# A streaming-encoder trunk on one core: four tiles side by side in the first pass, the first norm by tokens, a last tile split over fewer rows, and buffers at other places

## The chip, the cores and the metric

The kernel runs on one core of one Trainium2 chip. The metric is the device time of one execution in microseconds (us). Before the change the median of three runs is 1658.42 us (1656.04 to 1658.62).

## What is computed

One layer of a token mixer on x of 256 tokens and 2048 features, followed by an MLP and a last norm. Cut to its core the reference is:

```
h = rmsnorm(x, g1)
z = h @ w_in + b_in                      # 7 parts of 2048: xa, ya, cb, cc, cx, ga, gb
xa = rg_lru(causal_conv4(xa) + conv_a_b) # gates by 8 blocks of 256, a forward scan
out_a = (xa * gelu(ya)) @ w_pa
out_b = (cb * causal_conv3(cc * cx)) @ w_pb
x = x + (sigmoid(ga) * out_a + sigmoid(gb) * out_b) @ w_o
u = relu(rmsnorm(x, g2) @ w_mlp1) ** 2   # 8192 wide
out = rmsnorm(x + u @ w_mlp2, final_g)
```

Everything is float32.

## The kernel before

Features lie on the 128 partitions, tokens along the free side. x is kept as `x[128, 16, 256]`: 16 rows k of 128 features, 256 tokens each. Each operand of a product is split in two float32r parts, hi (a cast, on ACT) and lo (what the cast lost, on DVE); a buffer like `xg[128, 16, 2, 256]` holds both. A weight tile is 128 outputs wide; its weights for 8 rows k are a slab of 128 x 1024 numbers (512 KB). `Weights.make` loads a slab into a `raw` buffer with one DMA on SP's queue and splits it into `whi` and `wlo`; `take` keeps three slabs ahead of the one in use, in four buffers each. A row of a product is a pair of matmuls: hi weights against hi and lo data side by side (512 columns), lo weights against hi data (256 columns), both into one PSUM bank (`psz`, six of them). A tile of a z part is 16 such pairs, 32 for the second MLP product.

The tile framework puts the instructions of each engine in an order by priority; `high_priority(AHEAD)` draws the splits forward. Each engine then works through its own list in order, and so do the DMA queues.

The parts that the change touches:

- **The beginning.** x comes in eight pieces of two rows with quarters of two tiles' slabs between them (`load_x`, `W.make(2, 4, ...)`). The norm's factor is one number per token and is applied after the product (`z_done` multiplies by `rs`), so PE can start on x scaled by g1 alone. `first_pair` does the two xa tiles side by side, row by row; the two ya tiles follow one after the other from whole slabs; these four are the early tiles. `first_norm` squares x on ACT in eight parts, adds them up on DVE, sums over partitions with matmuls by `ones` (`total`), and takes the inverse root of 128 x 256 numbers (`rsqrt`).
- **The merged branches** `mg` (128 x 16 x 2 x 256, in a pool of its own, `big2`) are streamed by the w_o product (16 tiles) and, reused for `u`, by half of the rows of the second MLP product's second part (15 tiles and the last one). All other products but the small gate ones stream a `big` buffer, of which there are three.
- **The end.** The last tile (feature row 15, 32 rows k) is done in two halves of 128 tokens. After each half its squares complete the sum of squares of all features (`ssq` holds the others'), a short chain on one column gives the scale of its tokens (`scale_of`), a matmul spreads it over the partitions (`spread`), and `store` multiplies 16 feature rows by it and writes them out, 512 bytes for each feature and half.

Of the kernel before, what the change touches and what calls it, by code (L numbers as in the profile page):

```python
# [9 lines left out]
F32 = mybir.dt.float32  # L10
# [28 lines left out]
class Weights:  # L39
# [8 lines left out]
    def make(self, n=1, parts=1, before=None):  # L48

        nc = self.nc  # L50
        w = HALF * P // parts
        got = [(self.slabs[len(self.made) + m],
                self.raw_pool.tile([P, HALF * P], F32, name="raw"),
                self.hi_pool.tile([P, HALF * P], F32R, name="whi"),
                self.lo_pool.tile([P, HALF * P], F32R, name="wlo")) for m in range(n)]
        for i in range(parts):
            c = slice(i * w, (i + 1) * w)
            if before is not None:
                before(i)
            for src, raw, hi, lo in got:  # L60
                nc.sync.dma_start(raw[:, c], src[:, c])  # L61
                with self.tc.high_priority(AHEAD):
                    nc.scalar.copy(hi[:, c], raw[:, c])  # L63
                    nc.vector.tensor_tensor(lo[:, c], raw[:, c], hi[:, c].bitcast(F32), ALU.subtract)  # L64
        self.made += [(hi, lo) for _, _, hi, lo in got]
# [19 lines left out]
def trunk(ctx: ExitStack, tc: tile.TileContext, xT, par, w_in, w_lru, w_pa, w_pb, w_o, w_1, w_2, out):  # L85
# [40 lines left out]
    pr = keep.tile([P, NPAR], F32, name="pr")  # L126

# [18 lines left out]
    sink = keep.tile([P, 1], F32, name="sink")  # L146
    nc.scalar.copy(sink, eps)
# [21 lines left out]
    xg = big.tile([P, NT, 2, S], F32R, name="big")  # L169

# [76 lines left out]
    def first_pair():  # L247

        w = W.first(4)
        two = [psz.tile([P, 2, S], F32, name="psz") for _ in range(2)]  # L250
        for k in range(NT):
            for m in range(2):
                hi, lo = w[k // HALF * 2 + m]
                c = slice(k % HALF * P, (k % HALF + 1) * P)
                nc.tensor.matmul(two[m], hi[:, c], xg[:, k], start=k == 0, stop=False)  # L255
                nc.tensor.matmul(two[m][:, 1, :], lo[:, c], xg[:, k, 0, :], start=False, stop=k == NT - 1)
        return two

    early = first_pair() + [z_product() for m in range(2)]

    def first_norm(pool):
        parts = [pool.tile([P, 2, S], F32, name=n) for n in ("xc", "gy", "cb", "cc", "gate0", "gate1", "q", "v")]
        for k in range(HALF):
            nc.scalar.activation(parts[k], x[:, 2 * k:2 * k + 2, :], AF.Square, scale=pc("one", 0))
        n = HALF // 2
        while n:
            for k in range(n):
                nc.vector.tensor_tensor(parts[k], parts[k], parts[n + k], ALU.add)
            n //= 2
        rsqrt(rs, [parts[0][:, 0, :], parts[0][:, 1, :]])  # L270
# [3 lines left out]
    with tc.tile_pool(name="w1", bufs=1) as w1:  # L274
        first_norm(w1)
        for g in range(NB):
# [33 lines left out]
            if g == 0:  # L310
                decay()
# [34 lines left out]
    big2 = ctx.enter_context(tc.tile_pool(name="big2", bufs=1, reuse_waits="tile"))  # L346
    mg = big2.tile([P, NT, 2, S], F32R, name="mg")
# [43 lines left out]

    w = [W.take() for _ in range(4)]
    eye = pr[:, OFF["eye"]:OFF["eye"] + P]
    col = {}

    def sum_of(th):

        ps = psl.tile([P, 512], F32, name="psl")
        nc.tensor.matmul(ps[:, 0:1], ssq[:, th * P:(th + 1) * P], ones[:, 0:1], start=True, stop=False)
        return ps  # L400

    def half(th, between):
        c = slice(th * P, (th + 1) * P)
        ps = psz.tile([P, 2, S], F32, name="psz")
        for k in range(4 * HALF):
# [5 lines left out]
            nc.tensor.matmul(ps[:, :, :P], hi[:, b], a, start=k == 0, stop=False)  # L411
# [26 lines left out]
    def spread(d):  # L438

        ps = psl.tile([P, 1, 512], F32, name="psl")  # L440
        nc.tensor.matmul(ps[:, 0, :P], ones, d[:, :P], start=True, stop=True)
        return ps[:, :, :P]
# [64 lines left out]
```

## Time and profile before

| | |
|---|---|
| median of 3 runs | 1658.42 us (1656.04 to 1658.62) |
| the profiled execution, own time | 1657.99 us |
| its span, first to last instruction | 1656.1 us |
| PE busy | 1637.5 us (99%), 9490 matmuls |
| DVE, ACT busy | 68%, 52% |
| DMA | 312 MB, mean 189 GB/s |

The span is shorter than the execution's time by what lies around the first and last instruction. Times in rows are counted from the span's start. PE is TensorE's matmuls (their ends are modelled, so two that follow one another overlap in the rows, and their starts are the better measure), DVE VectorE, ACT ScalarE, SPq the DMA queue that SyncE issues. What stands in square brackets behind a row is the idle time of the engine ahead of it and what ended it.

### The profile page before, as it was taken

The page shows a single profiled execution, that of the slowest core. Times are in us where ns is not written, and L with a number is a line of the kernel's source. Part 1 is how long each engine was busy: PE and PEld are TensorE (multiplying, and loading weights), DVE is VectorE, ACT ScalarE, POOL GpSimd, SP SyncE. Part 2 cuts the span into 40 slices and gives each one's busy share as a digit, 9 for nine tenths or more (in the row PEclk, how much of TensorE's full clock was granted, in tenths as well). Part 3 has the DMA queues.
Part 4 walks back from the last instruction along what each step waited for, and adds up shares of the span by engine and source line. Part 5 has one row for each costly group of instructions (what it writes and reads, how often), then busy time and mean ns, then how long its engine had stood idle before and what let it go on. Part 6 is the DMA issues. An engine that isn't in the chain of part 4 may idle for free.

```text
span 1656.1 us, 24430 instructions
## 1 busy us (share of the span) xinstructions
PE 1637.5 (99%) x9490; PEld 1440.7 (87%) x9490; DVE 1130.7 (68%) x1645; ACT 867.7 (52%) x1275; POOL 3.4 (0%) x37
## 2 busy tenths in 40 slices
PE   8999999999999999999999999999999999999997
PEld 6888888888888888888888888888888888888886
DVE  6989779878977666666667666665555777755554
ACT  7666666666665444444455544444443444444443
POOL 0000000000000000000000000000000000000000
PEclk9999999999999999999999999999999999999998
DMA  8565555555555555555555555555555555555552
GB/s 257 181 192 190 191 192 190 187 192 192 186 186 193 190 191 191 191 191 190 190 183 189 185 189 190 189 191 190 190 191 190 191 190 191 188 188 188 189 190 90
DMA packets 91604, 312.21 MB, mean 189 GB/s; under 512 B 9952, under 2 KB 16224, under 8 KB 91488
## 3 DMA queue, kind: packets, MB, share of 16 engines
q1 hardware_dynamic: 91488, 310.66, 57.7%
q8 instruction: 74, 1.21, 0.3%
q14 instruction: 42, 0.34, 0.1%
HBM read 308.52 MB, written 2.10 MB: 188 GB/s over the span
## 4 chain that ended last, share of the span: by engine, by line
PE 97%; DMA 1%; DVE 1%; ACT 0%; SPq 0%; issue 0%; DVEq 0%; ACTq 0%
PE psz L225 62%; PE psz L226 32%; DMA raw<-w_in_s 1%; DVE wlo L64 1%; PE psz L411 0%; PE psl L319 0%; PE psl L320 0%; PE psl L321 0%; DMA pr<-par 0%; ACT whi L63 0%; PE psz L412 0%; DVE x L447 0%; SPq L61 0%; SPq L172 0%; PE psl L154 0%
## 5 line engine op out<-in xcount | busy, mean ns | idle before, releaser
L225 PE MATMUL psz<-big,whi 128*128 128x512 f32 x4048 | 1407.1, 392 | 1.6 <-ACT whi L63 1.2
L226 PE MATMUL psz<-big,wlo 128*128 128x256 f32 x4048 | 1133.5, 280 | 0.8 <-DVE wlo L64 0.8
L64 DVE TENSOR_TENSOR wlo<-raw,whi 128x1024 fp32r<-128x1024 f32 (+1 forms) x596 | 714.2, 1202 | 491.3 <-ACT whi L63 490.8
L63 ACT CAST whi<-raw 128x1024 fp32r<-128x1024 f32 (+1 forms) x596 | 615.5, 1034 | 757.2 <-issue 424.9
L225 PEld LDWEIGHTS psz<-big,whi 128*128 128x128 f32 x4048 | 760.8, 188 | 171.1 <-ACT whi L63 1.6
L226 PEld LDWEIGHTS psz<-big,wlo 128*128 128x128 f32 x4048 | 761.6, 188 | 1.1 <-DVE wlo L64 1.1
L225 PE MATMUL psz<-mg,whi 128*128 128x512 f32 x496 | 175.9, 399 | 0.0
L226 PE MATMUL psz<-mg,wlo 128*128 128x256 f32 x496 | 139.2, 281 | 0.0
L225 PEld LDWEIGHTS psz<-mg,whi 128*128 128x128 f32 x496 | 93.3, 188 | 23.1 <-DVE mg L134 0.2
L233 DVE TENSOR_TENSOR t<-psz,low 128x256 f32<-128x256 f32 x255 | 105.9, 418 | 0.0
L226 PEld LDWEIGHTS psz<-mg,wlo 128*128 128x128 f32 x496 | 93.9, 189 | 0.0
L231 ACT COPY low<-psz 128x256 f32<-128x256 f32 x255 | 92.1, 362 | 0.0
L238 DVE TENSOR_TENSOR t<-t,rs 128x256 f32<-128x256 f32 x112 | 47.2, 423 | 2.3
L373 DVE SCALAR_TENSOR_TENSOR s<-t 128x256 f32<-128x256 f32 x64 | 27.2, 425 | 2.1
L331 DVE RECIPROCAL q<-q 128x512 f32<-128x512 f32 x8 | 26.8, 3346 | 0.0
L287 DVE SCALAR_TENSOR_TENSOR xc<-xa,pr,xc 128x256 f32<-128x256 f32 x48 | 22.2, 479 | 0.0
L134 DVE TENSOR_TENSOR big<-s,big 128x256 fp32r<-128x256 f32 x48 | 20.1, 418 | 0.0
L255 PE MATMUL psz<-big,whi 128*128 128x512 f32 x32 | 14.1, 480 | 5.5 <-ACT whi L63 5.5
L133 ACT CAST big<-s 128x256 fp32r<-128x256 f32 x48 | 19.3, 402 | 0.0
L138 DVE SCALAR_TENSOR_TENSOR big<-x,pr,big 128x256 fp32r<-128x256 f32 x32 | 14.7, 481 | 4.7 <-ACT big L137 4.7
L319 PE MATMUL psl<-xs,whi 128*128 128x256 f32 x64 | 17.9, 280 | 0.0
L321 PE MATMUL psl<-xs,wlo 128*128 128x256 f32 x64 | 17.9, 280 | 0.0
(132 smaller groups left out, 552.2 us busy)
## 6 DMA issues: line engine op xcount, KB each, us to landing
raw<-w_s SPq DMA_DIRECT2D x256, 512.0 KB, 4.2
raw<-w_in_s SPq DMA_DIRECT2D x220, 512.0 KB, 3.8
raw<-w_pb_s SPq DMA_DIRECT2D x32, 512.0 KB, 3.5
raw<-w_pa_s SPq DMA_DIRECT2D x32, 512.0 KB, 3.6
raw<-w_o_s SPq DMA_DIRECT2D x32, 512.0 KB, 3.5
raw<-w_lru_s SPq DMA_DIRECT2D x8, 512.0 KB, 4.4
x<-xT SPq DMA_DIRECT2D x8, 256.0 KB, 4.6
raw<-w_in_s SPq DMA_DIRECT2D x16, 128.0 KB, 4.1
```

The source lines that it names most:

```text
L63: nc.scalar.copy(hi[:, c], raw[:, c])
L64: nc.vector.tensor_tensor(lo[:, c], raw[:, c], hi[:, c].bitcast(F32), ALU.subtract)
L133: nc.scalar.copy(dst[:, 0, :], src)
L134: nc.vector.tensor_tensor(dst[:, 1, :], src, dst[:, 0, :].bitcast(F32), ALU.subtract)
L225: nc.tensor.matmul(ps, hi[:, k * P:(k + 1) * P], a, start=i == 0, stop=False)
L226: nc.tensor.matmul(ps[:, 1, :], lo[:, k * P:(k + 1) * P], a[:, 0, :], start=False, stop=i == n - 1)
L231: nc.scalar.copy(low, ps[:, 1, :])
L233: nc.vector.tensor_tensor(t, ps[:, 0, :], low, ALU.add)
L238: nc.vector.tensor_tensor(t, t, rs, ALU.mult)
L287: nc.vector.scalar_tensor_tensor(c, xa[:, m, tap:tap + S], pc("ca_w", tap * NT + j), c, ALU.mult, ALU.add)
L331: nc.vector.reciprocal(q, q)
L373: nc.vector.scalar_tensor_tensor(v, t, 0.0, t, ALU.max, ALU.mult)
```

## The change

- **First pass.** Both xa and both ya tiles are made side by side (`first_four`): for each row k four pairs, into four PSUM banks. Their weights come in eight pieces, each two rows of x and the weights of four tiles for them (two DMAs of 256 KB), and are split into two `big` buffers, `fhi` and `flo`. Three slabs for the next tiles are loaded behind them.
- **x by tokens.** A second input, `xt`, holds x with tokens on the partitions. Behind the three slabs it is loaded in eight DMAs of 256 KB on SP's queue, into buffers of the pool `w1`, which is opened earlier for that. ACT squares each part and sums it along its row in the same instruction. The norm's factor is then worked out on 128 x 2 numbers and spread with two matmuls against the unit matrix. What the early tiles' drains need is issued after that (`issue_after(scaled)`).
- **Nine matmuls on `ones`** stand ahead of the first pass, their result unused.
- **The last tile** is done at full width over rows 0 to 13 and in halves over rows 14 to 31 (`SPLIT` = 18). The half's sum is added to x directly from PSUM, without the copy on ACT; the scale's column is spread by a matmul with the unit matrix instead of a product with it and a matmul by `ones`. The first half's stores are issued after the last half's adds, the last half's partly from ACT's queue.
- **Places.** Two tiles that nothing uses, `space` (104 columns) and `space2` (40 columns), move what is allocated behind them. As built, in bytes of a partition: the `raw`, `whi` and `wlo` buffers begin 512 higher (`whi` at 153,056, before 152,544), `mg` at 195,200 (before 194,528). The three `big` buffers stay at 16,512, 49,280 and 82,048.

```diff
+WAKE = 9
+SPLIT = 18
-          ("br", NT), ("bi", NT), ("lam", NT), ("cb_w", 3 * NT), ("one", 1), ("eye", P)]
+          ("br", NT), ("bi", NT), ("lam", NT), ("cb_w", 3 * NT), ("eye", P)]
...
+    def split(self, hi, lo, raw):
+        with self.tc.high_priority(AHEAD):
+            self.nc.scalar.copy(hi, raw)
+            self.nc.vector.tensor_tensor(lo, raw, hi.bitcast(F32), ALU.subtract)
...
+    keep.tile([P, 104], F32, name="space")
...
+    awake = psl.tile([P, 512], F32, name="psl")
+    for _ in range(WAKE):
+        nc.tensor.matmul(awake[:, :P], ones, ones, start=True, stop=True)
...
-    load_x(0, 2)
-    W.make(2, 4, lambda i: load_x(2 * i, 2) if i else None)
-    W.make(2, 4, lambda i: load_x(HALF + 2 * i, 2))
+    fhi = big.tile([P, NT // 2, 4, 2 * P], F32R, name="big")
+    flo = big.tile([P, NT // 2, 4, 2 * P], F32R, name="big")
+    for i in range(NT // 2):
+        load_x(2 * i, 2)
+        c, o = divmod(i, HALF // 2)
+        raw = rawp.tile([P, 4, 2 * P], F32, name="raw")
+        for q, z in enumerate((Z_XA, Z_YA)):
+            nc.sync.dma_start(raw[:, 2 * q:2 * q + 2, :],
+                              w_in[z:z + 2, c, :, o * 2 * P:(o + 1) * 2 * P].rearrange("m p n -> p m n"))
+            if i == 0:
+                W.split(fhi[:, i, 2 * q:2 * q + 2], flo[:, i, 2 * q:2 * q + 2], raw[:, 2 * q:2 * q + 2])
+        if i:
+            W.split(fhi[:, i], flo[:, i], raw)
+    W.ahead(LOOK)
+
+    places = ExitStack()
+    w1 = places.enter_context(tc.tile_pool(name="w1", bufs=1))
+    acc = keep.tile([P, 2, 4], F32, name="acc")
+    for i, n in enumerate(("xc", "gy", "cb", "cc", "gate0", "gate1", "q", "v")):
+        h, q = divmod(i, 4)
+        part = w1.tile([P, 2, S], F32, name=n)
+        nc.sync.dma_start(part, xt[h, :, q * 512:(q + 1) * 512])
+        nc.scalar.activation(part, part, AF.Square, accum_out=acc[:, h, q:q + 1])
...
+        four = [psz.tile([P, 2, S], F32, name="psz") for _ in range(4)]
         for k in range(NT):
+            c = slice(k % 2 * P, (k % 2 + 1) * P)
+            for m in range(4):
+                hi, lo = fhi[:, k // 2, m, c], flo[:, k // 2, m, c]
+                nc.tensor.matmul(four[m], hi, xg[:, k], start=k == 0, stop=False)
+                nc.tensor.matmul(four[m][:, 1, :], lo, xg[:, k, 0, :], start=False, stop=k == NT - 1)
+        return four
...
+        nc.vector.tensor_reduce(r, acc, mybir.AxisListType.X, ALU.add)
+        nc.vector.tensor_scalar(r, r, 1.0 / D, EPS, ALU.mult, ALU.add)
+        nc.scalar.activation(y, r, AF.Sqrt)
+        nc.vector.reciprocal(y, y)
+        nc.vector.tensor_tensor(m, r, y, ALU.mult)
+        nc.vector.scalar_tensor_tensor(m, m, -0.5, y, ALU.mult, ALU.mult)
+        nc.vector.scalar_tensor_tensor(m, m, 1.5, y, ALU.add, ALU.mult)
+        ps = psl.tile([P, 512], F32, name="psl")
+        for h in range(2):
+            nc.tensor.matmul(ps[:, h * P:(h + 1) * P], m[:, h:h + 1].broadcast_to([P, P]), eye, start=True, stop=True)
+        return nc.scalar.copy(rs, ps[:, :S]).ins
...
+    big2.tile([P, 40], F32, name="space2")
     mg = big2.tile([P, NT, 2, S], F32R, name="mg")
...
+    k0 = nk - SPLIT
+    got = []
+    t = added(rows(0, k0, slice(0, S)))
+    nc.vector.tensor_tensor(x[:, NT - 1, :], x[:, NT - 1, :], t, ALU.add)
+    sq0, _ = squared(0, rows(k0, nk, half(0), {nk - 6: lambda: got.append(begin(0))}))
+    sq1, done = squared(1, rows(k0, nk, half(1), {
+        k0 + 4: lambda: got.append(begin(1)), k0 + 8: lambda: got.append(scale(0, got[0], sq0)),
+        nk - 2: lambda: got.append(spread(got[2][0]))}))
+    with tc.issue_after(done):
+        store(0, got[3], 0, (4, 4), (nc.sync,))
+    m, done = scale(1, got[1], sq1)
+    with tc.issue_after(done):
+        store(0, got[3], 8, (4,), (nc.sync,))
+    by = spread(m)
+    with tc.issue_after(store(1, by, 0, (2,), (nc.scalar,))):
+        store(0, got[3], 12, (4,), (nc.sync,))
+    store(1, by, 2, (5, 5, 4), (nc.sync, nc.scalar))
```

On PE, at the start of the program, the pairs of the two xa tiles (`psz_196`, `psz_197`) alternate before:

```order
L255 MATMUL psz_196<-big_89,whi_97 128x512
L256 MATMUL psz_196<-big_89,wlo_98 128x256
L255 MATMUL psz_197<-big_89,whi_100 128x512
L256 MATMUL psz_197<-big_89,wlo_101 128x256
L255 MATMUL psz_196<-big_89,whi_97 128x512
L256 MATMUL psz_196<-big_89,wlo_98 128x256
L255 MATMUL psz_197<-big_89,whi_100 128x512
L256 MATMUL psz_197<-big_89,wlo_101 128x256
```

After the change (`big_101` is `fhi`, `big_102` `flo`, `big_90` `xg`; `psz_237` to `psz_240` are the four tiles):

```order
L164 MATMUL psl_91<-ones_81 128x128 x9
L270 MATMUL psz_237<-big_90,big_101 128x512
L270 MATMUL psz_238<-big_90,big_101 128x512
L271 MATMUL psz_237<-big_90,big_102 128x256
L271 MATMUL psz_238<-big_90,big_102 128x256
L270 MATMUL psz_239<-big_90,big_101 128x512
L270 MATMUL psz_240<-big_90,big_101 128x512
L270 MATMUL psz_237<-big_90,big_101 128x512
L271 MATMUL psz_239<-big_90,big_102 128x256
L271 MATMUL psz_240<-big_90,big_102 128x256
L271 MATMUL psz_237<-big_90,big_102 128x256
```

The nine matmuls on `ones` stand ahead, four tiles take turns in place of two, and in the first piece, which is split in two parts, hi matmuls of two tiles go before their lo ones.

On PE, at the first norm, before (`psz_454` is the first cb tile, the two L154 matmuls sum the squares of x):

```order
L225 MATMUL psz_454<-big_89,whi_304 128x512
L226 MATMUL psz_454<-big_89,wlo_305 128x256
L225 MATMUL psz_454<-big_89,whi_304 128x512
L226 MATMUL psz_454<-big_89,wlo_305 128x256
L154 MATMUL psl_398<-xc_375,ones_81 128x256 x2
L225 MATMUL psz_454<-big_89,whi_304 128x512
L226 MATMUL psz_454<-big_89,wlo_305 128x256
```

After (`psz_481` is the second cb tile, the L290 matmuls spread the factors `m`):

```order
L241 MATMUL psz_481<-big_90,whi_199 128x512
L242 MATMUL psz_481<-big_90,wlo_200 128x256
L241 MATMUL psz_481<-big_90,whi_199 128x512
L242 MATMUL psz_481<-big_90,wlo_200 128x256
L241 MATMUL psz_481<-big_90,whi_199 128x512
L242 MATMUL psz_481<-big_90,wlo_200 128x256
L241 MATMUL psz_481<-big_90,whi_199 128x512
L290 MATMUL psl_381<-pr_80,m_373 128x128 x2
L242 MATMUL psz_481<-big_90,wlo_200 128x256
L241 MATMUL psz_481<-big_90,whi_199 128x512
```

The norm's matmuls moved from behind two pairs of the first cb tile to behind three pairs and a hi matmul of the second, 17 pairs further in the work that follows the early tiles.

On DVE, at the end of the program, before, from the first half's stores (L447, `psl_15850`) on:

```order
L447 TENSOR_TENSOR x_79<-x_79,psl_15850 128x5x128 x2
L447 TENSOR_TENSOR x_79<-x_79,psl_15850 128x3x128 x2
L416 TENSOR_TENSOR low_15876<-low_15876,x_79 128x128
L417 TENSOR_TENSOR x_79<-psz_15791,low_15876 128x128
L429 TENSOR_SCALAR cr1_15888<-psl_15844 128x1
L430 RECIPROCAL cy1_15889<-cy1_15889 128x1
L431 TENSOR_TENSOR cm1_15890<-cr1_15888,cy1_15889 128x1
L432 SCALAR_TENSOR_TENSOR cm1_15890<-cm1_15890,cy1_15889 128x1
L433 SCALAR_TENSOR_TENSOR cm1_15890<-cm1_15890,cy1_15889 128x1
L435 TENSOR_SCALAR t_15897<-pr_80,cm1_15890 128x128
L447 TENSOR_TENSOR x_79<-x_79,psl_15899 128x2x128
L447 TENSOR_TENSOR x_79<-x_79,psl_15899 128x4x128
```

After, from the last half's adds (L447 and L448) on (L480 are the products of the stores, of the first half by `psl_15817`, of the last by `psl_15844`):

```order
L447 TENSOR_TENSOR x_79<-psz_15772,x_79 128x128
L448 TENSOR_TENSOR x_79<-psz_15772,x_79 128x128
L480 TENSOR_TENSOR x_79<-x_79,psl_15817 128x4x128 x2
L465 TENSOR_SCALAR cr1_15833<-psl_15781 128x1
L466 RECIPROCAL cy1_15834<-cy1_15834 128x1
L467 TENSOR_TENSOR cm1_15835<-cr1_15833,cy1_15834 128x1
L468 SCALAR_TENSOR_TENSOR cm1_15835<-cm1_15835,cy1_15834 128x1
L469 SCALAR_TENSOR_TENSOR cm1_15835<-cm1_15835,cy1_15834 128x1
L480 TENSOR_TENSOR x_79<-x_79,psl_15817 128x4x128
L480 TENSOR_TENSOR x_79<-x_79,psl_15844 128x2x128
L480 TENSOR_TENSOR x_79<-x_79,psl_15817 128x4x128
L480 TENSOR_TENSOR x_79<-x_79,psl_15844 128x5x128 x2
```

The first half's four store products moved from ahead of the last half's adds to behind them, two before the last half's scale chain, one behind it, and one between the last half's own stores.

## Rows read from the trace of the kernel before

**Rows 1.** The page: busy time of each engine with its share of the span and its instructions, and the chain that ended last by engine.

```profile
PE 1637.5 (99%) x9490; PEld 1440.7 (87%) x9490; DVE 1130.7 (68%) x1645; ACT 867.7 (52%) x1275; POOL 3.4 (0%) x37
...
PE 97%; DMA 1%; DVE 1%; ACT 0%; SPq 0%; issue 0%; DVEq 0%; ACTq 0%
```

**Rows 2.** PE in order of time, 4 to 49 us: start us, length us, engine, line, operation, out<-in, shape, count, and idle time ahead with what ended it.

```profile
4.98 0.79 PE L255 MATMUL psz<-big,whi 128*128 128x512 f32 x1 [4.98 <-ACT whi L63]
...
11.24 0.63 PE L255 MATMUL psz<-big,whi 128*128 128x512 f32 x1
...
11.88 0.63 PE L255 MATMUL psz<-big,whi 128*128 128x512 f32 x1
...
21.69 0.51 PE L225 MATMUL psz<-big,whi 128*128 128x512 f32 x1 [1.24 <-ACT whi L63]
22.95 0.58 PE L226 MATMUL psz<-big,wlo 128*128 128x256 f32 x1 [0.75 <-DVE wlo L64]
...
37.12 1.10 PE L154 MATMUL psl<-xc,ones 128*128 128x256 f32 x4 [0.77 <-DVE sd L203]
...
48.47 0.39 PE L225 MATMUL psz<-big,whi 128*128 128x512 f32 x1
```

**Rows 3.** Two stretches of the beginning: length, busy us of PE, PEld, DVE, ACT and POOL with the instructions in brackets, granted clock, DMA share, GB/s.

```profile
8.00:22.00 14.00, 12.76 (x61) 10.75 (x59) 10.24 (x28) 12.31 (x30) 0.00 (x0) 1.00 0.97 322
22.00:36.00 14.00, 13.25 (x67) 11.45 (x67) 11.22 (x13) 10.65 (x15) 0.00 (x0) 0.88 0.78 254
```

**Rows 4.** All engines in order of time, 6 to 22 us: the split of x's second piece on ACT and DVE, and the split of a whole slab.

```profile
6.75 0.91 ACT L137 ACTIVATE big<-x,pr 128x256 fp32r<-128x256 f32 x2 [0.24 <-DMA x<-xT]
...
7.29 0.89 DVE L138 SCALAR_TENSOR_TENSOR big<-x,pr,big 128x256 fp32r<-128x256 f32 x2 [0.32 <-ACT big L137]
...
20.61 1.03 ACT L63 CAST whi<-raw 128x1024 fp32r<-128x1024 f32 x1
...
21.67 1.23 DVE L64 TENSOR_TENSOR wlo<-raw,whi 128x1024 fp32r<-128x1024 f32 x1 [2.74 <-ACT whi L63]
```

**Rows 5.** ACT in order of time, 18 to 37 us: a square of 128 x 512 and a load of the function table.

```profile
18.75 0.72 ACT L264 ACTIVATE xc<-x,pr 128x512 f32<-128x512 f32 x1 [0.44 <-DMA pr<-par]
...
36.64 1.28 ACT L161 ACT_TABLE_LOAD   x1
```

**Rows 6.** The page's costliest groups: the hi matmuls by the buffer that they stream, with count, busy us and mean ns of one.

```profile
L225 PE MATMUL psz<-big,whi 128*128 128x512 f32 x4048 | 1407.1, 392 | 1.6 <-ACT whi L63 1.2
...
L225 PE MATMUL psz<-mg,whi 128*128 128x512 f32 x496 | 175.9, 399 | 0.0
```

**Rows 7.** PE in order of time in the w_o stage (streaming `mg`) and in the first MLP product (streaming `big`): in each the first and the last of 17 hi matmuls that follow one another.

```profile
873.19 0.40 PE L225 MATMUL psz<-mg,whi 128*128 128x512 f32 x1
...
878.85 0.40 PE L225 MATMUL psz<-mg,whi 128*128 128x512 f32 x1
...
1000.05 0.39 PE L225 MATMUL psz<-big,whi 128*128 128x512 f32 x1
...
1005.60 0.39 PE L225 MATMUL psz<-big,whi 128*128 128x512 f32 x1
```

**Rows 8.** PE in order of time in the last tile: the matmul on `ssq`, two hi matmuls of the first half with 13 between them, and the last half's last lo matmul.

```profile
1633.10 0.38 PE L399 MATMUL psl<-ones,ssq 128*128 128x1 f32 x2 [0.33 <-DVE ssq L191]
...
1633.61 0.33 PE L411 MATMUL psz<-big,whi 128*128 128x256 f32 x1
...
1636.81 0.33 PE L411 MATMUL psz<-big,whi 128*128 128x256 f32 x1
...
1645.01 0.22 PE L412 MATMUL psz<-big,wlo 128*128 128x128 f32 x1
```

**Rows 9.** ACT, DVE and SP in order of time behind the last half: adds, scale chain, product with the unit matrix, first store's product and its DMA's issue.

```profile
1645.27 0.27 ACT L414 COPY low<-psz 128x128 f32<-128x128 f32 x1 [5.30 <-PE psz L412]
1645.57 0.29 DVE L416 TENSOR_TENSOR low<-low,x 128x128 f32<-128x128 f32 x1
1645.96 0.29 DVE L417 TENSOR_TENSOR x<-psz,low 128x128 f32<-128x128 f32 x1
...
1647.07 0.26 ACT L428 ACTIVATE cy<-psl,eps 128x1 f32<-128x1 f32 x1
...
1647.44 0.15 DVE L430 RECIPROCAL cy<-cy 128x1 f32<-128x1 f32 x1
...
1648.02 0.16 DVE L433 SCALAR_TENSOR_TENSOR cm<-cm,cy 128x1 f32<-128x1 f32 x1
1648.21 0.29 DVE L435 TENSOR_SCALAR t<-pr,cm 128x128 f32<-128x128 f32 x1
...
1649.45 0.42 DVE L447 TENSOR_TENSOR x<-x,psl 128x256 f32<-128x256 f32 x1 [0.95 <-PE psl L441]
...
1649.89 0.37 SPq L448 DMA_DIRECT2D outT<-x  x1
```

**Rows 10.** Four stretches of the end, columns as in rows 3.

```profile
1644.80:1648.40 3.60, 0.82 (x6) 0.58 (x5) 2.18 (x10) 1.24 (x4) 0.00 (x0) 0.91 1.01 284
1648.40:1650.80 2.40, 0.77 (x2) 0.50 (x2) 1.45 (x4) 0.00 (x0) 0.00 (x0) 0.50 0.04 12
1650.80:1654.60 3.80, 0.00 (x0) 0.00 (x0) 1.13 (x2) 0.00 (x0) 0.00 (x0) 0.50 0.95 271
1654.60:1656.10 1.50, 0.00 (x0) 0.00 (x0) 0.00 (x0) 0.00 (x0) 0.00 (x0) 0.50 0.04 11
```

More of the change, by code (lines that the diff above doesn't have):

```diff
@@ L46, in __init__, with make @@
         self.at = 0
[L48 to L65, printed above, removed]
+    def split(self, hi, lo, raw):
+        with self.tc.high_priority(AHEAD):
+            self.nc.scalar.copy(hi, raw)
+            self.nc.vector.tensor_tensor(lo, raw, hi.bitcast(F32), ALU.subtract)
+    def make(self):
+        raw = self.raw_pool.tile([P, HALF * P], F32, name="raw")
+        hi = self.hi_pool.tile([P, HALF * P], F32R, name="whi")
+        lo = self.lo_pool.tile([P, HALF * P], F32R, name="wlo")
+        self.nc.sync.dma_start(raw, self.slabs[len(self.made)])
+        self.split(hi, lo, raw)
+        self.made.append((hi, lo))
     def ahead(self, n):
@@ L84, in trunk @@
 @with_exitstack
-def trunk(ctx: ExitStack, tc: tile.TileContext, xT, par, w_in, w_lru, w_pa, w_pb, w_o, w_1, w_2, out):
+def trunk(ctx: ExitStack, tc: tile.TileContext, xT, xt, par, w_in, w_lru, w_pa, w_pb, w_o, w_1, w_2, out):
     nc = tc.nc
@@ L103, in trunk @@
         for z in (Z_XA, Z_YA, Z_CB, Z_CC, Z_CX):
-            if g == 0 and z == Z_XA:
-                slabs += [w_in[z + m, c] for c in range(2) for m in range(2)]
-            else:
+            if g > 0 or z not in (Z_XA, Z_YA):
                 unit(w_in, z + 2 * g, 2)
@@ L245, in z_tile, with first_four @@
         z_done(z_product(), j, dst, func)
-    def first_pair():
-        w = W.first(4)
-        two = [psz.tile([P, 2, S], F32, name="psz") for _ in range(2)]
+    def first_four():
+        four = [psz.tile([P, 2, S], F32, name="psz") for _ in range(4)]
         for k in range(NT):
[L252 to L270, printed above, removed]
+            c = slice(k % 2 * P, (k % 2 + 1) * P)
@@ L392, in trunk, with rows @@
     w = [W.take() for _ in range(4)]
[L393 to L403, printed above, removed]
+    nk = 4 * HALF
+    def rows(k0, k1, c, between=()):
         ps = psz.tile([P, 2, S], F32, name="psz")
-        for k in range(4 * HALF):
+        for k in range(k0, k1):
             if k in between:
@@ L432, in scale_of @@
         nc.vector.scalar_tensor_tensor(m, m, -0.5, y, ALU.mult, ALU.mult)
-        nc.vector.scalar_tensor_tensor(m, m, 1.5, y, ALU.add, ALU.mult)
-        d = wk.tile([P, S], F32, name="t")
-        nc.vector.tensor_scalar(d[:, :P], eye, m, None, ALU.mult)
-        return d
[L438 to L442, printed above, removed]
-    def store(th, by, at, parts):
-        for n in parts:
-            xp = x[:, at:at + n, th * P:(th + 1) * P]
-            nc.vector.tensor_tensor(xp, xp, by.broadcast_to([P, n, P]), ALU.mult)
-            nc.sync.dma_start(out[th, :, at:at + n, :], xp)
-            at += n
```

84 lines of the change are left out of this document (52 added, 32 removed).

## The prediction

> **What bounds the kernel now.** The page comes first. TensorE counts as busy for 99% of the span and holds 97% of the chain that ended last [rows 1]. So between the ends nothing else matters: there the kernel is as long as its matmuls, and only their own pace can be changed. The second view is PE in order of time over the first 48 us [rows 2]. The first matmul starts at 4.98, the pairs (one hi, one lo) come 0.64 us apart at first (11.24 to 11.88, the pace of 1.2 GHz, though the granted clock column stands at 1.00 there [rows 3], before its first recorded change), PE waits 1.24 us until 21.69 and again until 22.95 for whole slabs to be split, and at 37.12 for the sum of squares. The seventh z tile, the first one after the two xa, two ya and two cb tiles (I call its beginning the cc start), begins at 48.47. The six before it, 16 pairs each, at the pace of an undisturbed stage, 0.347 us (1000.05 to 1005.60 is 16 pairs) [rows 7], are 33.3 us, so 15.2 us of the beginning are not matmul at full pace. The third view is the groups by operand: hi matmuls that stream `mg` take 399 ns, those that stream a `big` buffer 392, with the same weights' buffers behind them [rows 6]. The fourth is the end: after the last half matmul (1645.23) the span goes on for 10.9 us, of which 4.2 are a chain through ACT, DVE and PE to the first store and the rest is writing out [rows 8 to 10].
>
> **First pass and norm.** What moves is the order of data. Before, the DMA engines brought two tiles' slabs beside x and then whole slabs; now each of eight pieces is two rows of x (0.262 MB) and four tiles' weights for them (0.524 MB), 0.786 MB, for eight pairs, 2.78 us of PE. I reckon when each piece lands. Before, the second part of x was used at 6.75 [rows 4], and what was queued up to it, 0.795 MB, is just what the new first piece has. From 8 to 22 us the engines moved 322 GB/s at a share of 0.97 [rows 3], so a piece comes each 2.44 us: the second at 9.2, the eighth at 23.8. After landing, ACT needs 1.03 us for the hi part and then DVE 1.23 us for the lo part (the new calls are as wide as those rows) [rows 4], so the lo parts stand 2.3 us after landing, 11.5 for the second piece. With the split of x ahead of it ACT spends some 1.9 us a piece and DVE 2.1, both under 2.44. PE runs 8 pairs a piece: the second ends at 14.1, the third has its lo part at 13.9, and from there PE is the slower one: 14.1 + 6 × 2.78 = 30.8 us for the end of the pass. In front, nine matmuls on `ones` keep PE at work from about 1.0 until the first piece. They cost nothing, since PE had nothing to do there; what they buy is that the pace has risen by 11.5. If it hasn't, each us longer at 0.64 a pair costs about half a us.
>
> Next come three ready slabs (1.57 MB), then the second copy of x by tokens (2.10 MB, new traffic), then the rest of the parameters, then the fourth slab. At 322 GB/s the slabs are in at 28.7, in time for 30.8, and the tokens at 35.2. The norm now is: square 0.72, table load 1.28 [rows 5], square root 0.26, four DVE steps on two columns (0.8, as the one-column steps at the end [rows 9]), so the two norm matmuls can start at 38.3. They stand three and a half pairs into the third slab, where PE arrives at 30.8 + 5.55 + 1.2 = 37.55: a stall of 0.8, and about 0.5 for the fp32 matmuls themselves. Four and a half pairs and the fourth slab (landed 37.5, split by 40) follow: the cc start is at 38.35 + 0.5 + 1.55 + 2.78 = 43.2 instead of 48.47, **5.3 us** less. Queued behind that wait on PE is only the rest of the tile; on ACT the fourth slab's split stands behind the square root, and it is needed at 40.4. The two removed early products lie inside the 48.47. The cc tile takes the PSUM bank of the first xa tile; its drain follows the copy of `rs` (about 39.5) and is done by 41, two us early. The older norm's DVE adds and its wide reciprocal go away; they were covered by PE at work, and so are the delayed drains. Bounds: with no stall, 42.4, a gain of 6.1. With the later traffic at the 254 GB/s of 22 to 36 us [rows 3], the tokens land 14.4 us after 23.8, at 38.2, the cc start is 46.2 and the gain 2.3. In that window issues waited for free buffers, while the new ones have eight buffers of their own, so I go with 322.
>
> **The places.** As built, `mg` began 32 bytes past a multiple of 64 and the `big` buffers on one; now both are on one. Pairs on `mg` came 0.354 us apart (873.19 to 878.85 is 16), those on `big` 0.347 [rows 7]; the difference is in the hi matmul [rows 6]. 496 pairs × 6.9 ns = **3.4 us**, if place is the cause. It is the operand that differs between these rows, not the stage, since the last projection mixes both. Bounds 0 and 3.5. Against it speaks the Trainium skill, "TensorE: Matmul & The Clock Gate", Part 2 (What happens when you issue a matmul): PE reads SBUF by two independent ports, so that loading the next weights takes nothing from the running matmul. By that rule the place would be worth nothing and the sum would be 3.4 us longer; the rows show a price that it doesn't name. The weights' buffers move by 512 bytes. Inside a slab each row k is 512 bytes further than the one before, and the 16 pairs from 1000.05 on, two slabs, hold the pace all the same; I take 0. The first pass now has its weights in `big` buffers too, on a multiple of 64 like the data they meet; if that cost the same 6.9 ns, 64 pairs would be 0.4 us.
>
> **The end.** Of the last tile 14 of 32 rows are now done at full width and 18 in halves. A half pair takes 0.2286 us (1633.61 to 1636.81 is 14), so 28 half pairs, 6.40 us, become 14 full ones, 4.86: 1.54 less. The wait of 0.33 at 1633.10 for `ssq` [rows 8] goes, as that matmul now comes some 7 us after the tile's start: together 1.87. The last half needs 1.1 us from its end to its square sum and meets it 2.0 us on, so scale(0) doesn't stall PE.
>
> After PE the copy of 0.3 on ACT and the product with `eye` (0.3) are gone [rows 9], but all stores of the first half (1.05 MB), which had been running since 1644.8, now wait for the last half's adds. With both halves, 2.10 MB remain after PE's end. The first store's product ends about 1.4 us after it (two dependent adds 0.72, a product of 512 columns some 0.65); data flow 0.95 after an issue (1649.89, flowing at 1650.8); at 284 GB/s [rows 10] 2.10 MB take 7.4 us; small gaps 0.2. So the writing ends 9.9 us after PE where it was 9.4 (1654.6): 0.5 lost. The scale chain is no longer what ends last. **1.4 us** remain (bounds 0.4, with a full us more without data, and 2.2 if the writing were no slower than before).
>
> **Sum.** 5.3 + 3.4 + 1.4 = 10.1 us off the profiled execution's own 1657.99 (span 1656.1, 1.9 around it), which is 0.4 under the median 1658.42: **1647.9 us**.
>
> **Rivals.** (a) The place isn't the cause, `mg` pairs stay at 0.354: 1651.3. For it speaks that no row shows one buffer at two places. It is also where the rule of the Trainium skill weighed above (the two read ports) leads. (b) The second copy of x comes late because the DMA engines don't hold 322 GB/s: the norm matmuls stand at the head of PE's queue until 41.3, 1650.9. For it: 254 GB/s in the later window, and eight more transfers in the busiest stretch; against it, that window's issues waited. Both together: 1654.3. (c) Slower: the weights' new place costs what `mg`'s did, because moving data and weights now meet badly. Then 4,048 pairs on `big` × 6.9 ns = 27.9 us are added: 1675.8; from 2.5 ns a pair on the change loses. Against it, the even pace from row to row. That the change does nothing isn't a rival, since the waits at 21.7, 22.95 and 37.1 can't recur where they stood.
>
> **How the numbers follow.** Forecast 0.65; (a) 0.14; (b) 0.13; both 0.04; (c) 0.04. The forecast's own range is its bounds with runs 1.3 us apart on either side, 1645.2 to 1650; reaching to (a) and (b) gives 1645.2 to 1651.8, which leaves out some 0.15. About 0.2% (3.3 us) is what a measurement of this kernel can tell from no change. Faster by more: all but (c) and half of "both" with a margin for what I overlook, 0.92; same 0.04; slower 0.04.
>
> **What would show it.** The first pass's pairs at 0.347 from about 12 us and ending near 31; one wait of PE under 1 us at the norm matmuls; the cc start near 43. Hi matmuls on `mg` at 392 ns. Half matmuls 1.9 us shorter in all, and writing without a break until about 9.9 us after PE's end. Wrong would be: pairs at 0.64 beyond 14 us, a norm wait of several us, `mg` still at 399, or hi matmuls on `big` over 394.

## The result, and the profile after

The changed kernel takes **1646.6 us** (median of 4 runs, 1646.1 to 1646.88), the kernel before 1658.04 beside it: a ratio of 0.9933, 95% interval 0.992 to 0.9945. That is 11.4 us less; the prediction was 1647.9 in a range of 1645.2 to 1651.8. The profiled execution took 1646.88 us with a span of 1645.0, against 1657.99 and 1656.1. Its 11.1 us come apart at two places that both traces have, the cc start and the start of the last tile. Before, the first cb pair, with which the early tiles are over, and the last tile began here (PE in order of time):

```profile
35.49 0.39 PE L225 MATMUL psz<-big,whi 128*128 128x512 f32 x1
...
1628.96 0.28 PE L411 MATMUL psz<-mg,whi 128*128 128x256 f32 x1
```

| stretch | before | after | less | predicted |
|---|---|---|---|---|
| span's start to cc start | 48.47 | 42.57 | 5.90 | 5.3 |
| cc start to the last tile | 1580.49 | 1577.03 | 3.46 | 3.4 |
| last tile's start to span's end | 27.14 | 25.40 | 1.74 | 1.4 |

Of the 5.90, 4.47 lie ahead of the first cb pair (35.49 before, 31.02 now) and 1.43 at the norm behind it. The places are tested below by kernels that differ in nothing else. No run takes back the new first pass, the norm by tokens or the new last tile alone: what these are worth is read from the two traces.

The page of the changed kernel, for [rows 1, 6] (the chain is still PE's, and the hi matmuls on `mg` now take what those on `big` take):

```profile
PE 1632.0 (99%) x9480; PEld 1439.1 (87%) x9480; DVE 1123.6 (68%) x1628; ACT 867.3 (53%) x1272; POOL 3.4 (0%) x37
...
PE 99%; DVE 1%; DMA 0%; issue 0%; SPq 0%; DVEq 0%; ACT 0%
...
L241 PE MATMUL psz<-big,whi 128*128 128x512 f32 x4016 | 1394.0, 392 | 0.4 <-DVE big L125 0.4
...
L241 PE MATMUL psz<-mg,whi 128*128 128x512 f32 x496 | 172.8, 392 | 0.0
```

PE in order of time, for [rows 2]: the end of the first pass, the norm matmuls with the pairs around them, and the cc start.

```profile
30.31 0.40 PE L270 MATMUL psz<-big 128*128 128x512 f32 x1
...
30.67 0.40 PE L270 MATMUL psz<-big 128*128 128x512 f32 x1
...
31.02 0.39 PE L241 MATMUL psz<-big,whi 128*128 128x512 f32 x1
...
37.84 0.61 PE L290 MATMUL psl<-pr,m 128*128 128x128 f32 x4
38.20 0.36 PE L242 MATMUL psz<-big,wlo 128*128 128x256 f32 x1
...
42.57 0.39 PE L241 MATMUL psz<-big,whi 128*128 128x512 f32 x1
```

No bracket stands behind the 37.84: PE didn't wait there. The chain of the norm on ACT and DVE shows why, its last step done 1.2 us earlier:

```profile
33.63 0.63 ACT L197 ACTIVATE v<-v 128x512 f32<-128x512 f32 x1
...
34.37 1.28 ACT L283 ACT_TABLE_LOAD   x1
35.67 0.20 ACT L283 ACTIVATE y<-r 128x2 f32<-128x2 f32 x1
...
36.49 0.16 DVE L287 SCALAR_TENSOR_TENSOR m<-m,y 128x2 f32<-128x2 f32 x1
```

The two stretches of [rows 3] (same columns): PE busy throughout, and the DMA engines faster than the 322 and 254 GB/s before.

```profile
8.00:22.00 14.00, 14.00 (x73) 12.15 (x72) 11.44 (x18) 11.18 (x19) 0.00 (x0) 0.88 1.07 359
22.00:36.00 14.00, 14.00 (x81) 12.20 (x81) 6.76 (x10) 11.22 (x24) 0.00 (x0) 1.00 0.98 342
```

The end, for [rows 8 to 10], all engines in order of time: the last tile's first matmul, PE's last lo matmul, adds and store products on DVE, the first issue.

```profile
1619.60 0.39 PE L438 MATMUL psz<-mg,whi 128*128 128x512 f32 x1
...
1633.45 0.22 PE L439 MATMUL psz<-big,wlo 128*128 128x128 f32 x1
...
1633.71 0.29 DVE L447 TENSOR_TENSOR x<-psz,x 128x128 f32<-128x128 f32 x1 [1.46 <-PE psz L439]
...
1634.24 1.27 DVE L480 TENSOR_TENSOR x<-x,psl 128x512 f32<-128x512 f32 x2
...
1634.95 5.70 SPq L481 DMA_DIRECT2D outT<-x  x6
...
1637.13 3.08 DVE L480 TENSOR_TENSOR x<-x,psl 128x256 f32<-128x256 f32 x5 [0.29 <-PE psl L474]
```

And three stretches of the writing, columns as in [rows 3]:

```profile
1635.70:1637.60 1.90, 0.80 (x2) 0.50 (x2) 1.54 (x6) 0.00 (x0) 0.00 (x0) 0.66 0.91 255
1637.60:1643.40 5.80, 0.00 (x0) 0.00 (x0) 2.62 (x4) 0.00 (x0) 0.00 (x0) 0.50 0.98 278
1643.40:1645.00 1.60, 0.00 (x0) 0.00 (x0) 0.00 (x0) 0.00 (x0) 0.00 (x0) 0.50 0.00 1
```

PE ends at 1633.67 and the writing at 1643.4, 9.7 us later (9.4 before).

### The profile page after: what moved, and what is told of

It is laid out like the page before. It is cut to its first block, busy times and chain, and to the rows that moved or that the text cites. A ratio compares the mean times of both kernels' runs of the same rounds, so it can differ in the third digit from the quotient of the medians.

```text
span 1645.0 us, 24379 instructions
## 1 busy us (share of the span) xinstructions
PE 1632.0 (99%) x9480; PEld 1439.1 (87%) x9480; DVE 1123.6 (68%) x1628; ACT 867.3 (53%) x1272; POOL 3.4 (0%) x37
## 4 chain that ended last, share of the span: by engine, by line
PE 99%; DVE 1%; DMA 0%; issue 0%; SPq 0%; DVEq 0%; ACT 0%
PE psz L241 63%; PE psz L242 32%; PE psz L270 1%; PE psz L438 1%; PE psz L271 1%; PE psl L351 0%; PE psl L352 0%; PE psl L353 0%; DMA raw<-w_in_s 0%; PE psz L439 0%; DVE x L480 0%; DVE wlo L53 0%; DVE v L373 0%; PE psl L474 0%; ACT big L52 0%
## 5 line engine op out<-in xcount | busy, mean ns | idle before, releaser
L241 PE MATMUL psz<-big,whi 128*128 128x512 f32 x4016 | 1394.0, 392 | 0.4 <-DVE big L125 0.4
L53 DVE TENSOR_TENSOR wlo<-raw,whi 128x1024 fp32r<-128x1024 f32 x576 | 703.2, 1223 | 480.0 <-ACT whi L52 479.5
L52 ACT CAST whi<-raw 128x1024 fp32r<-128x1024 f32 x576 | 606.3, 1053 | 740.4 <-issue 404.1
L242 PEld LDWEIGHTS psz<-big,wlo 128*128 128x128 f32 x4016 | 753.8, 188 | 0.0
L270 PE MATMUL psz<-big 128*128 128x512 f32 x64 | 23.2, 417 | 1.5 <-ACT big L52 1.5
L351 PE MATMUL psl<-xs,whi 128*128 128x256 f32 x64 | 17.9, 279 | 0.0
L352 PE MATMUL psl<-xs,whi 128*128 128x256 f32 x64 | 17.9, 279 | 0.0
```

Of the source, the lines that this page charges most:

```text
L52: self.nc.scalar.copy(hi, raw)
L53: self.nc.vector.tensor_tensor(lo, raw, hi.bitcast(F32), ALU.subtract)
L241: nc.tensor.matmul(ps, hi[:, k * P:(k + 1) * P], a, start=i == 0, stop=False)
L242: nc.tensor.matmul(ps[:, 1, :], lo[:, k * P:(k + 1) * P], a[:, 0, :], start=False, stop=i == n - 1)
L270: nc.tensor.matmul(four[m], hi, xg[:, k], start=k == 0, stop=False)
```

## Experiments on the places

The **distance** below is the address of the moving data less that of the weights (hi and lo buffers lie 16,384 apart, so it is the same for both), modulo 512 bytes. Before, `mg` was at 0 and `big` at 160; in the changed kernel all are at 160, but the first pass, whose weights lie in `big` buffers, is at 0. The pace is the mean time from one hi matmul to the next.

**`mg` put back.** Without `space2`:

```diff
-    big2.tile([P, 40], F32, name="space2")
```

> The changed kernel without the 160 bytes ahead of mg: mg lies 32 bytes past a multiple of 64 again, and 0 bytes from the weights' buffers modulo 512 (both at 480). Everything else stays. Place theory, in any form: hi matmuls on mg back at 399 ns, pairs 0.3535 us apart, 496 x 6.9 ns = 3.4 us more, about 1650.0. Rival (the place is not the cause, something else in the change made mg faster): hi on mg stays 392 ns, pairs 0.3467, 1646.6.

1650.42 us (1650.06 to 1650.6), and on the page:

```profile
L241 PE MATMUL psz<-mg,whi 128*128 128x512 f32 x496 | 175.9, 399 | 0.0
```

The place is the cause: 3.8 us come back. **The other way round**, the kernel before with `mg` moved alone:

```diff
+    big2.tile([P, 8], F32, name="space2")
     mg = big2.tile([P, NT, 2, S], F32R, name="mg")
```

> The kernel before, with nothing changed but 32 bytes ahead of mg, so that mg begins on a multiple of 64 (0 modulo 512, the weights still at 480). Place theory: hi matmuls on mg 392 ns and pairs 0.3467, 3.4 us less, about 1654.6. Rival (in the changed kernel the gain came from elsewhere): 399 ns, 1658.0.

1654.17 us beside 1657.68, ratio 0.998 (0.9971 to 0.999): 3.5 us less. The 16 pairs of [rows 7] on `mg` took 5.66; here, 5.55:

```profile
872.65 0.39 PE L225 MATMUL psz<-mg,whi 128*128 128x512 f32 x1
...
878.20 0.39 PE L225 MATMUL psz<-mg,whi 128*128 128x512 f32 x1
```

So rival (a) is out. Which property of the place? **`mg` elsewhere on 32 past a multiple of 64:**

```diff
-    big2.tile([P, 40], F32, name="space2")
+    big2.tile([P, 48], F32, name="space2")
```

> The changed kernel with mg 32 bytes further on: 32 past a multiple of 64 like before the change, but at 160 modulo 512, where the weights are at 480. Two theories of which place counts. Own place (moving data 32 past a multiple of 64 is slow): hi on mg 399 ns, 1650.0. Relation modulo 64 (data and weights in the same class modulo 64 are slow): also 399 ns, 1650.0. Relation modulo 512 (slow only where data and weights have the same place modulo 512): 392 ns, 1646.6.

1649.96 us, `mg` pairs 0.3533 (distance 192). So the theory that only the same place modulo 512 is slow is out. **The weights moved:**

```diff
-    keep.tile([P, 104], F32, name="space")
+    keep.tile([P, 160], F32, name="space")
```

> The changed kernel with the weights' buffers 224 bytes further: at 192 modulo 512, a multiple of 64, as the big buffers are (128 modulo 512); mg is at 352, 32 past a multiple of 64. Own place of the data: big pairs 0.3467, mg pairs 0.3535, 1650.0. Weights on a multiple of 64 are slow by themselves (which would explain the first pass): all 4,512 pairs 0.3535, 31.1 us more, 1677.7. Relation modulo 64: big slow, mg fast, 4,016 x 6.9 ns = 27.7 us more, 1674.3 (the price of rival (c)). Relation modulo 512: all fast, 1646.6.

**1673.03 us** (1672.74 to 1674.33), 26.4 more than the changed kernel and slower than before (ratio 1.0096, 1.0079 to 1.0112). In the w_in stage 16 pairs on `big` took 5.65 instead of 5.55 us, and the hi matmuls on `mg`, now the ones 32 past a multiple of 64, stayed fast. PE in order of time, and then the page:

```profile
137.95 0.40 PE L241 MATMUL psz<-big,whi 128*128 128x512 f32 x1
...
143.60 0.40 PE L241 MATMUL psz<-big,whi 128*128 128x512 f32 x1
```

```profile
L241 PE MATMUL psz<-big,whi 128*128 128x512 f32 x4016 | 1420.3, 398 | 0.1
...
L241 PE MATMUL psz<-mg,whi 128*128 128x512 f32 x496 | 173.0, 392 | 0.0
```

The granted clock is 1.00 over that stage in both kernels, so it isn't the clock, and it isn't the data's own place: it is where data and weights lie to each other. This is rival (c), made. **The weights on exactly the place of `big`:**

```diff
-    keep.tile([P, 104], F32, name="space")
+    keep.tile([P, 144], F32, name="space")
```

> The changed kernel with the weights' buffers 160 bytes further: at 128 modulo 512, exactly the place of the big buffers; mg is at 288, 32 past a multiple of 64. Own place of the data: big fast, mg slow, 1650.0. Weights on a multiple of 64 slow by themselves: all pairs 0.3535, 1677.7. Relation, modulo 64 or modulo 512: big slow, mg fast, 1674.3. If it comes out at 1674 while the kernel with the weights at 192 stays at 1646.6, the modulus is 512 and rival (c) of the prediction was one choice of a number away.

All theories fell: 1654.22 us, spread over 1648.16 to 1655.1 in seven runs. In the profile `big` ran at 0.3467 until 1450 us and at 0.3529 in the last projection; grouped by stretch (100 to 480 us, then 1470 to 1600), the hi matmuls on `big`:

```profile
L241 PE MATMUL psz<-big,whi 128*128 128x512 f32 x1040 | 360.9, 391 | 0.0
...
L241 PE MATMUL psz<-big,whi 128*128 128x512 f32 x191 | 67.9, 398 | 0.0
```

The same code on the same addresses thus runs at either pace, and changes between stages. **Three distances in one kernel**, by 32 bytes behind each `big` buffer (here and in the next, each `big` tile is a view on a longer one):

```diff
+PAD = 8
+        t = big.tile([P, NT * 2 * S + PAD], F32R, name="big")
-    keep.tile([P, 104], F32, name="space")
+    keep.tile([P, 128], F32, name="space")
-    big2.tile([P, 40], F32, name="space2")
+    big2.tile([P, 64], F32, name="space2")
```

> The changed kernel with 32 bytes behind each of the three big buffers, so that they begin at 128, 160 and 192 modulo 512, and the weights' buffers at 160: three distances between data and weights in one kernel, -32, 0 and +32, and mg at 416, a distance of 256. What the last four kernels suggest: data and weights in the same class modulo 64 cost 6.6 to 6.9 ns a pair, other classes nothing, and exactly the same place modulo 512 goes either way from run to run. By this -32 and +32 run at 0.3467, mg (256) at 0.3533 (3.3 us more), and the buffer at 0 (some 480 pairs) at either pace (up to 3.3 us), so 1649.9 to 1653.2. Rival (the distance is counted modulo 512 or 128, and only near 0 or 64 is slow): mg stays at 0.3467, 1646.6 to 1649.9; if nearness counts, -32 and +32 would be slow too, some 3,200 pairs, over 1667.

1662.37 us: outside what both gave. `xg` and `xh` (the data of the w_in stage and of the first MLP product, both in the first `big` buffer) ran at 0.3508 and 0.3533, though -32 is in the same class modulo 64 as the fast 160. The buffers at 0 and +32 ran at 0.347, `mg` at 0.3529 in the w_o stage and 0.347 later. **A rule formed from this, on new distances:**

```diff
+PAD = 48
+        t = big.tile([P, NT * 2 * S + PAD], F32R, name="big")
```

> The changed kernel with 192 bytes behind each big buffer, which puts xg and xh at 128 modulo 512, the second big buffer at 320, the third at 0, mg at 192, and the weights' buffers at 32. The runs so far: stretches at a distance (data less weights) of 32 modulo 128 have all run at 0.3467 to 0.3471 a pair; stretches at multiples of 64 ran slow or, in some executions, fast; one at -32 (96 modulo 128) ran now slow, now fast. If the rule is 32 modulo 128: the second buffer (distance 288) and mg (160) at 0.3467; xg and xh (96) and the third (-32) slow at least in part, up to 0.3533 for some 3,450 pairs, so over 1650 and up to 1669.4. Rival (only the class modulo 64 counts, and the uneven pace at -32 came from the weights' place at 160 itself): all of them at 0.3467, 1646.6.

1659.61 us (1658.67 to 1660.83). Two tiles of the second part of the MLP that follow one another, of 16 pairs each, the first on the buffer at 288 (5.55 us), the next on the one at -32 (5.65):

```profile
1111.79 0.39 PE L252 MATMUL psz<-big,whi 128*128 128x512 f32 x1
...
1117.34 0.39 PE L252 MATMUL psz<-big,whi 128*128 128x512 f32 x1
...
1117.69 0.39 PE L252 MATMUL psz<-big,whi 128*128 128x512 f32 x1
...
1123.34 0.39 PE L252 MATMUL psz<-big,whi 128*128 128x512 f32 x1
```

All stretches together, by distance modulo 128 (pace in us a pair, first pass left out):

| modulo 128 | distances tried | pace |
|---|---|---|
| 32 | 32, 160, 288, 416 | 0.3467 to 0.3474; to 0.3480 where its tiles take turns with a slow buffer's |
| 64 | 192, -64 | 0.3517 to 0.3533 |
| 96 | 96, -32 | 0.3477 to 0.3533, mostly 0.350 or more |
| 0 | 0, 256 | 0.3467 to 0.3533, by stage and by run |

The rule held in every stage behind the first pass. In the first pass, where hi and lo weights lie in two `big` buffers at two distances, it did not: with -32 and -64 (the kernel with three distances) and with 320 and 128 (the kernel just shown) the pairs ran at 0.3467, and in a later kernel (the last of the experiments on the end) with 288 and 160, each 32 modulo 128, at 0.3499. Why any of it is so no run shows; what can be said is that a slow stretch costs up to 6.6 ns for each hi and lo pair, and that behind the first pass 32 modulo 128 was never slow.

## Experiments on the beginning

**Without the nine matmuls on `ones`:**

```diff
-WAKE = 9
+WAKE = 0
```

> The changed kernel without the nine matmuls on ones. In the kernel before, PE ran from 4.98 us on and its pairs went from 0.64 to 0.35 us apart at about 12.8, 7.8 us later. My theory: the rise comes as much later as PE's work begins: first matmul at 6.6, rise at about 14.3 instead of 11.5, so 2.8 us at 0.64 instead of 0.35 a pair, 1.3 us lost, about 1647.9. Rival (the nine matmuls change nothing, since the first pass waits for data anyway): 1646.6, the pass ends at 31.0 all the same.

1647.26 us (1647.0 to 1647.35), 0.7 more than with nine. The theory fell: the first matmul came at 5.66 and the pairs reached full pace at about 12, not at 14.3. The pass ends at 31.15.

**With twelve of them:**

```diff
-WAKE = 9
+WAKE = 12
```

> The changed kernel with twelve matmuls on ones instead of nine: they end near 6.4, where the first pass begins, so the gap of 1.5 us between 5.03 and 6.57 closes. Without any of them the pace rose at 12.1 instead of 11.5 and the time was 0.7 us longer. If the gap puts the rise off: it comes up to 1.5 us earlier, 0.3 to 0.7 us less, about 1646.1. Rival (the gap doesn't matter, and the three more only stand in front of the first piece): rise at 11.5, 1646.6 to 1647.0.

1646.19 us (1646.05 to 1646.34). PE is at full pace from 7.1 us on, and doesn't fall back. In the changed kernel, where PE stood idle from 5.03 to 6.57, it was at full pace from 6.9, fell to half (0.64 us a pair) at 8.1 and rose at 11.5 to 11.8 (granted clock 0.54 from 8 to 10 us, 0.50 from 10 to 11). But now PE waits for data, so the pass still ends at 30.48:

```profile
10.58 1.19 PE L270 MATMUL psz<-big 128*128 128x512 f32 x4 [0.62 <-ACT big L52]
```

So the time hardly depends on the gap. That closing it kept the pace up isn't shown: in two profiled kernels with nine matmuls, and so with a gap, the pace didn't fall back either (last section). Seven other kernels with nine matmuls ended the pass at 30.1 to 30.9, so the 0.4 us by which it is ahead of the changed kernel can't be told from chance; the 0.7 lost without any can, barely.

**Each transfer of x by tokens twice:**

```diff
-        nc.sync.dma_start(part, xt[h, :, q * 512:(q + 1) * 512])
+        for _ in range(2):
+            nc.sync.dma_start(part, xt[h, :, q * 512:(q + 1) * 512])
```

> The changed kernel with each of the eight transfers of x by tokens made twice, 2.1 MB more in the busiest stretch: rival (b) of the prediction, made on purpose. In the changed kernel the last DVE step before the norm matmuls ends at 36.65 and PE takes them at 37.84, so there is a slack of 1.2 us. At the 342 GB/s of that stretch the tokens come 6.1 us later: PE then waits 4.9 us at the norm matmuls, 1651.5. Rival (the norm isn't on the path, or its transfers find free room): no wait of PE there, 1646.6.

1658.67 us: all of the gain gone. PE waited 7.8 us at the norm matmuls, and its clock fell (0.81 from 36 to 48.8; pairs 0.64 apart from 50.6 to about 54). ACT's last square, PE's norm matmuls and the cc start, in order of time:

```profile
45.71 0.63 ACT L198 ACTIVATE v<-v 128x512 f32<-128x512 f32 x1 [1.29 <-DMA v<-xt]
...
48.79 1.22 PE L291 MATMUL psl<-pr,m 128*128 128x128 f32 x4 [7.81 <-DVE m L288]
...
54.61 0.39 PE L242 MATMUL psz<-big,whi 128*128 128x512 f32 x1
```

The cc start is 12.0 us later than in the changed kernel: 1.5 are a first pass that ended at 32.47, 7.8 the wait, 2.8 the matmuls behind it, most of them at half pace. The last square begins 12.1 us later (33.63 there), where 6.1 were expected.

The waits of SP's queue from 15 to 50 us (total us, times, longest us):

```profile
SPq L197 <- DMA gate<-xt: 4.7, 2, 4.4
...
SPq L197 <- DMA xc<-xt: 3.9, 1, 3.9
```

They are why the tokens come so much later: the second copy into a buffer waits on SP's queue until the first has landed, which holds up what stands behind it. That late tokens hold PE up at the norm matmuls, as rival (b) has it, is shown; the price here is in part that of this edit's own waits.

## Experiments on the end

**Four planes stored early:**

```diff
-    sq1, done = squared(1, rows(k0, nk, half(1), {
+    last = rows(k0, nk, half(1), {
...
+    store(0, got[3], 0, (4,), (nc.sync,))
+    sq1, done = squared(1, last)
     with tc.issue_after(done):
-        store(0, got[3], 0, (4, 4), (nc.sync,))
+        store(0, got[3], 4, (4,), (nc.sync,))
```

> The changed kernel, but the first four planes of the first half are scaled and stored as soon as their scale is spread, ahead of the last half's two adds, instead of behind them. The prediction put the price of holding these stores back at 0.5 us (writing that ends 9.9 us after PE instead of 9.4). From the trace of the changed kernel: the scale is there at about 1633.1, one scaling of four planes takes 0.63 us, so its store is issued at 1633.8 instead of 1634.95, the last half's adds come at most 0.1 us later, and if writing is what ends last, the end comes 1.0 to 1.1 us earlier: 1645.6. Rival (the last half's chain sets the end, and DVE's extra work ahead of it counts): 1646.6 to 1647.3.

1646.71 us (1646.1 to 1646.75): no change, the rival. The first product moved up to 1632.97 and data flowed 1 us sooner, but ran dry, and the last half's products came no sooner: 3.65 us behind PE's end (1633.34 here), where it was 3.46 in the changed kernel. DVE in order of time, then three stretches (the DMA share is the column before GB/s):

```profile
1632.97 0.69 DVE L480 TENSOR_TENSOR x<-x,psl 128x512 f32<-128x512 f32 x1 [1.06 <-PE psl L474]
...
1636.99 3.08 DVE L480 TENSOR_TENSOR x<-x,psl 128x256 f32<-128x256 f32 x5 [0.29 <-PE psl L474]
```

```profile
1634.70:1636.80 2.10, 0.91 (x4) 0.68 (x4) 1.38 (x7) 0.53 (x2) 0.00 (x0) 0.58 0.83 244
1636.80:1637.60 0.80, 0.16 (x1) 0.00 (x0) 0.61 (x2) 0.00 (x0) 0.00 (x0) 0.50 0.00 0
1637.60:1643.20 5.60, 0.00 (x0) 0.00 (x0) 2.47 (x4) 0.00 (x0) 0.00 (x0) 0.50 0.98 280
```

The us won in front came back as 0.8 us without data. What flows behind this gap is more than the last half: 5.6 us at 280 GB/s are 1.57 MB, 1.05 of the last half and 0.52 of the first, planes 8 to 15, whose products stand behind the last half's scale chain in this kernel too. No run stored those earlier. **With the first pass's weights moved as well:**

```diff
+PAD = 32
+    fhi = weights_of(big_tile(24))
+    flo = weights_of(big_tile(24))
-    keep.tile([P, 104], F32, name="space")
+    keep.tile([P, 8], F32, name="space")
```

(`big_tile(24)` is a view that begins 24 columns, 96 bytes, into a buffer 32 columns longer.)

> The kernel with the early store and, for the first pass, the weights' buffers of the four tiles at another place against x (distances 288 and 160 modulo 512 instead of 0). In the changed kernel's profile the first pass ran at 0.3535 a pair, in four other kernels with the same places at 0.3467. Expected: first pass at 0.3467 (0.3 us less than in the profile of the changed kernel, nothing against its runs that were fast there), and 1.0 us from the stores: 1645.4. Rival (as for the early store): 1646.4 to 1647.1.

1646.6 us (1646.06 to 1646.97). The first pass ran at 0.3499, not 0.3467, so the distances 288 and 160, both 32 modulo 128, weren't fast there; why stays open. No version here beats the changed kernel by more than its runs differ.

## Why the prediction was right, and where it was off

**First pass.** Right: it ended at 31.02, predicted 30.8, without a wait behind 12 us. The nine matmuls on `ones` were to keep PE at work until the first piece, but were over at 5.03, 1.5 us ahead of it. The bound of 0.4 us for weights in `big` buffers, taken as nothing, came true in this profile: 44 pairs from 15.1 on at 0.3535, 0.3 us. In seven other profiled kernels with this step at distance 0 it ran at 0.3466 to 0.3473, in one more at 0.3531: not a price but a draw. The reading that all pairs at the beginning rise once, by 11.5, was too simple (above).

**Norm.** The step that was off most: a stall of 0.8 us was predicted and none came. The DMA rate was the term: 322 GB/s were taken, 359 and 342 were measured, so the last square began at 33.63, the two norm matmuls could have begun at 36.7 instead of 38.3, and PE came at 37.84 (predicted 37.55). The other kernel's rate was not a limit of the engines, as 359 shows; what makes the new transfers faster no run shows. With 1.2 us to spare rival (b) was nearer than its 0.13 seemed to say: 0.4 MB more on the way (1.2 us at 342 GB/s) would have used it up.

**Places.** The size was right (3.4; 3.46, 3.5 and 3.8 in three comparisons), the reason half right. "Before 32 past a multiple of 64, now on one" describes what was done; but `mg` at 32 past one is slow with the weights at 480 (hi 397 to 399 ns) and fast with them at 192 or 128 (392). The prediction's "I take 0" for the weights' own move of 512 bytes was right since the distance modulo 512 didn't change; moved by 224 more they cost 26.4 us, close to the 27.9 of rival (c). The argument given against (c), the even pace from row to row, only shows that steps of 512 cost nothing, and says nothing on a shift of another size; (c) was ruled out by a fact that I hadn't looked at, and that it did not come true was luck. Before, the 15 tiles that alternate `mg` and `big` had even the `big` pairs at 0.348; they came down too, by some 0.3 us. The Trainium skill, "TensorE: Matmul & The Clock Gate", Part 2 (What happens when you issue a matmul), has the running matmul lose nothing to the weights' load because PE reads SBUF by two independent ports; here the pace of the same matmuls differs by 2% with the distance of the two operands, and the measurement decides. Whether the distance acts on the reading of the operands or on something else no run shows.

**End.** PE's part is 14.07 us from the tile's start instead of 16.27: 2.20 less, where 1.87 was predicted. The wait for `ssq` was mis-sized: the row's 0.33 is what PE stood idle, but from the hi matmul ahead of it to the one behind it 0.97 us pass, against 0.42 at the other small matmuls, so 0.55 went with it; the rest is half pairs that took 0.229 to 0.235. The writing's end 9.7 us after PE's (predicted 9.9) was right in size. Its stated cause, that the first half's stores are held back, is shown only in part. Of the four groups of planes, storing the first one earlier gains nothing. But the writing without a break from 1637.6 on (5.8 us) has 0.52 MB of the first half in it, 1.9 us at 278 GB/s, behind a chain that is shorter than before (first product of the last half 3.46 us behind PE's end instead of 4.22); whether these could be stored ahead of it wasn't tried.

## What to carry to other kernels

In a kernel whose pace is the matmul's, look at the mean time from hi matmul to hi matmul by buffer: two paces for one shape can come from the operands' places, and a pad of 224 bytes cost 1.6% of the time here. Compare distances between operands, not one operand's alignment, and measure every pair of buffers again after each move of an allocation: the rule of 32 modulo 128 is one kernel's, and its first pass doesn't follow it. A wait can cost more than the idle time that its row shows (0.55 us for 0.33 here), and a start moved up gains nothing where the supply behind it doesn't follow.

## What was not expected of the hardware

- Pairs of the same shape at the same addresses ran at 0.3467 or 0.3533 us (distance 0), changing at stage boundaries within one execution, and between executions (1648.16 to 1655.1 us). A third, even pace of 0.350 was seen at 96 (`xg` and `xh` in the last kernel of the places) and in the first pass with weights at 288 and 160.
- PE's pace in the first 12 us differed between nine profiled kernels that have the same code there (nine matmuls on `ones` until 4.8 to 5.2): full from 6.2 on at the latest in two; half until 9.5 to 10.4 in three; full, then half from about 8 to 11 or 12, in three; full until 11.6 and then half until 15.1 in one. The first real matmul came 0.4 to 0.8 us behind the last on `ones` in the first two and the last, 0.8 to 1.8 us behind it in the six others, so the gap alone doesn't tell the courses apart.
- The time with all of it stays nearly the same, since data comes no faster: the first pass ended at 30.1 to 31.2 in ten profiled kernels, at 32.1 in the one whose pace fell at 11.6, and at 32.5 in the one with x by tokens twice, whose first matmul came at 7.6.
